# A decoder layer on one core: pre-formed weight sums paced by length, and one more pair split ahead of the last sums

## The chip, the cores and the metric

The kernel runs on one core of a Trainium2 chip. A core has TensorE (PE, the matrix unit; PEld is its weight load), VectorE (DVE), ScalarE (ACT), GpSimd (POOL) and SyncE (SP, which only issues transfers); 16 DMA engines move data between the device memory (HBM) and the on-chip memory. The metric is the device time of one execution in microseconds (us). Three executions of the kernel before took 1059.58, 1060.62 and 1060.71 us; the median is 1060.62.

## The reference

One layer on 256 tokens of 2048 numbers, all in float32:

```
h = rmsnorm(x, pre_mix_g);  proj = h @ w_in                        # 2048 x 4368
o_a = sliding-window attention (16 heads), o_b = forgetting attention (16 heads)
mix = [rmsnorm(o_a), rmsnorm(o_b)] @ w_out                          # 2048 x 2048
x = x + rmsnorm(mix, post_mix_g)
h = rmsnorm(x, pre_ffn_g)
gate, val = split(causal_dwconv(h @ w_up, conv_w, conv_b))          # 2048 x 11264
y = (gelu(gate) * val) @ w_down                                     # 5632 x 2048
out = x + rmsnorm(y, post_ffn_g)
```

## The kernel before, in words

**Weights.** They stream from HBM once, in raw tiles of 128 x 1024 float32 (512 KB, five buffers). TensorE multiplies in a reduced float32 format, so each raw tile is split in two: ACT casts it to a high half (`whi`), DVE subtracts that from the raw tile and writes the low half (`wlo`). This is a *split*; a product of two split numbers takes three matrix products (high x high, high x low, low x high) or, where both halves of the activations lie side by side, two. `w_load` issues the load of a raw tile on SP (L90) and counts it in `loads`.

**Stages.** (1) The input projection and both attentions, to about 290 us. (2) The output projection and the mixing norm: for each half of the tokens (t = 0, 1) DVE adds the two groups' products (L767), ACT squares and sums the result (L768), POOL multiplies it by the norm's gain (L769), POOL computes `rmix` = 1/rms with a power (L214), DVE adds the scaled mix to x (L787) and TensorE transposes the new x for the next projection (L794). (3) The up projection of the first 22 of 44 blocks of the feed-forward width, with convolution and gelu, then the down projection of these blocks in two passes over the output columns; then the same for the second 22 blocks. The end is the last norm.

**Weight sums.** In the down projection, six of eleven pairs of 128-row blocks per half (`FAST`) are multiplied with seven block products in place of eight (a Strassen scheme, `seven`). It needs sums of blocks of `w_down`. These sums are made in HBM in the background: `make_sums` gives, for each half and pair, eight steps. Four are plain copies (`put`, issued on SP, L80) and four are transfers that add into their destination (`add`, issued on POOL, L83). In the first half, the last four steps cover half as many columns. `w_load` issues these 96 steps in a fixed order: before, after the twelfth load, at five of every thirteen loads one step is taken off the list, whatever its length. During the passes no step is issued (`paused`).

**Order.** TensorE's order is written by hand. In stage (2) around the mixing norm, and in the passes, ACT and DVE (and POOL at the norm) also run in the order of the code; elsewhere a scheduler sets it. Instructions on one engine start in order, and a transfer issued on POOL waits in POOL's queue for what it reads.

**The last pass** (second half, columns 1024 to 2047) handles the pairs in the order 0, 2, 4, 1, 5, 6, 7, 3, 8, 9, 10. The last three (8, 9, 10: `HOLD`) are *held*: their products are done at the very end, output block by output block, so that each block's norm work can start early. After the last fast pair (7), `ahead` splits the next pairs, `add_early` adds the four early products on DVE (L1162 to L1169, the *early sums*), and then the remaining held pairs are split. POOL's gain multiplications (L1253) and DVE's last sums (L1240, L1229) follow.

Of the kernel before, what the change touches and what calls it, by code (L numbers as in the profile page):

```python
# [12 lines left out]
ALU = mybir.AluOpType  # L13
# [11 lines left out]
NEG = -1e30  # L25
FHALF = 22
HOLD = 3
SKIP = 12
FAST = (0, 2, 4, 5, 6, 7)


# [1 line left out]
def hybrid_layer(ctx: ExitStack, tc: tile.TileContext, x, pre_mix_g, w_in, b_forget, sinks,  # L33
# [3 lines left out]
    pe, act, dve, pool, sp = nc.tensor, nc.scalar, nc.vector, nc.gpsimd, nc.sync  # L37
# [12 lines left out]
    def bank(tag="acc"):  # L50
        return ps.tile([P, 512], F32, tag=tag, bufs=4, name="bank_" + tag)
# [13 lines left out]
    UNIT = 1024  # L65
    WB = 5

    pair_sums, sum_steps, loads, paused = {}, [], [0], [False]

    def make_sums(half, u):  # L70
        k = half * FHALF + 2 * u
        chunks = slice(0, 2) if half else slice(0, 1)
        t13, t24 = (tc.dram_tile([P, D], F32, name=n) for n in ("t13", "t24"))
        pair_sums[half, u] = t13, t24
        (t1, t3), (t2, t4), (b11, b12), (b21, b22) = (
            [w.rearrange("p (s x c) -> p s x c", s=2, x=2)[:, :, x, :] for x in range(2)]
            for w in (t13, t24, *(w_down[(k + a) * P:(k + a + 1) * P, :] for a in range(2))))

        def put(to, src, ch=slice(0, 2)):
            return lambda: sp.dma_start(to[:, ch, :], src[:, ch, :])  # L80

        def add(to, src, ch=slice(0, 2)):
            return lambda: pool.dma_start(to[:, ch, :], src[:, ch, :], accum_op=ALU.add)  # L83

        return [put(t1, b11), put(t3, b22), add(t1, b12), add(t3, b12), put(t2, b22, chunks),
                put(t4, b21, chunks), add(t2, t1, chunks), add(t4, t2, chunks)]

    def w_load(src, a, c, pin=False):
        raw = wp.tile([P, UNIT], F32, tag="raw", bufs=5, name="raw")
        i = sp.dma_start(raw[:, :a * c].rearrange("p (a c) -> p a c", a=a), src)  # L90
        if pin:
            tc.keep_in_program_order(i)
        loads[0] += 1
        if loads[0] > SKIP and loads[0] * 5 % 13 < 5 and sum_steps and not paused[0]:
            tc.keep_in_program_order(sum_steps.pop(0)())
        return raw, a, c

    last = []
# [55 lines left out]
    def w_rows(w, k0, a, c0, c):  # L154
        return w[k0 * P:(k0 + a) * P, c0:c0 + c].rearrange("(a p) c -> p a c", p=P)
# [190 lines left out]
    with tc.tile_pool(name="mixp", bufs=1) as mp:  # L346
# [407 lines left out]
        hold = tc.tile_pool(name="hold", bufs=1)  # L754
# [61 lines left out]
        def out_cols(n, t, cs):  # L816
            b = bank()
            for k, hi, lo in kept[n]:
# [7 lines left out]
        order = tc.manual_schedule(engines={mybir.EngineType.Activation, mybir.EngineType.DVE,  # L826
                                            mybir.EngineType.Pool})
# [50 lines left out]
    with tc.tile_pool(name="ffn", bufs=1) as fp:  # L878
# [132 lines left out]
        def product(b, lh, ll, rhs, cols, first, last, to=None):  # L1011
            hi, lo = rhs
            for i, (a, r) in enumerate(((lh, hi), (lh, lo), (ll, hi))):
                pe.matmul(b[:, to] if to else b, a, r[:, cols], start=(first and i == 0),  # L1014
                          stop=(last and i == 2))

        def column_pass(G, sums, weights, some, order, k00, c0, load, parts, hold=1):

            left, right = slice(0, 512), slice(512, UNIT)
            ready_sums = k00 or c0 == 0  # L1020
            fast = [u for u in order if u in some]
            plain = [u for u in order[:-hold] if u not in some]
            ready, started, held, banks = {}, set(), [], []

            def of(k, t):
                return G[k][:, t * P:(t + 1) * P], G[k][:, 256 + t * P:256 + (t + 1) * P]

            def first(bk):
                new = id(bk) not in started
                started.add(id(bk))  # L1030
                return new

            def prepare(u):
                k = k00 + 2 * u
                if u not in some:
                    return [parts(load(w_rows(w_down, k + a, 1, c0, UNIT)), UNIT)
                            for a in range(2)]
                b11 = parts(load(w_rows(w_down, k, 1, c0, 512)), 512)
                w13, w24 = (w[:, c0:c0 + UNIT].rearrange("p (a c) -> p a c", a=1)
                            for w in weights[u])  # L1040
                r13 = load(w13)
                r2 = load(w_rows(w_down, k + 1, 1, c0, UNIT))
                f13 = parts(r13, UNIT)
                if ready_sums:
                    r24 = load(w24)
                else:
                    r24 = r13
                    dve.tensor_tensor(r24[:, left], r2[:, right], r13[:, left], op=ALU.add)
                    dve.tensor_tensor(r24[:, right], r2[:, left], r24[:, left], op=ALU.add)
                b2 = parts(r2, UNIT)  # L1050
                return b11, f13, b2, parts(r24, UNIT)

            def ahead(*us):
                for u in us:
                    ready[u] = prepare(u)

            def seven(u, forms, m1, m5, m7, m6, p2, p3, p4):
                k, end = 2 * u, u == fast[-1]
                b11, f13, b2, f24 = forms

                def s_of(j):
                    return of(k, 1) if j == 3 else [sums[u][:, i * 384 + j * P:i * 384 + (j + 1) * P]
                                                    for i in range(2)]

                steps = [(m1, of(k, 0), b11, left), (m5, s_of(3), f13, left),
                         (m7, s_of(0), f13, right), (p2, of(k + 1, 0), b2, left),
                         (p3, s_of(2), b2, right), (m6, s_of(1), f24, left),
                         (p4, of(k + 1, 1), f24, right)]
                if u == fast[0]:
                    steps = steps[0:3] + steps[5:] + steps[3:5]  # L1070
                for bk, a, b, cols in steps:
                    product(bk, *a, b, cols, first(bk), end and bk in (m1, m5, m7, m6))

            def run(add_early):
                early, late = ([bank(tag) for _ in range(4)] for tag in ("acc", "att"))
                banks.extend(zip(late, (0, 0, 1, 1), (left, right, left, right)))
                for i, u in enumerate(order):
                    forms = ready.pop(u) if u in ready else prepare(u)
                    if u in some:
                        seven(u, forms, *early, *late[:3])  # L1080
                        if u == fast[-1]:
                            ahead(*order[i + 1:i + 3])
                            add_early(*early)
                    elif i >= len(order) - hold:
                        held.extend((2 * u + a, forms[a]) for a in range(2))
                    else:
                        for a in range(2):
                            for bk, t, cols in banks:
                                product(bk, *of(2 * u + a, t), forms[a], cols, first(bk),
                                        hold > 1 and bk is late[3] and a == 1 and  # L1090
                                        u == plain[-1])
                return late

            def block(i, bk=None, cols=None):
                b, t, c = banks[i]
                for n, (k, w) in enumerate(held):
                    product(bk or b, *of(k, t), w, cols or c, bk is not None and n == 0,
                            n == len(held) - 1, cols and slice(cols.start - 512, cols.stop - 512))

            return ahead, run, block  # L1100

        raw_turns, split_turns, cycles = [], [], [None, None]

        def load(src):
            if not raw_turns:
                raw_turns.extend(cycles[0])
            raw, c = raw_turns.pop(0), src.shape[-1]
            if raw is None:
                return w_load(src, 1, c)[0]
            sp.dma_start(raw[:, :c].rearrange("p (a c) -> p a c", a=1), src)  # L1110
            return raw

        def parts(src, n):
            if not split_turns:
                split_turns.extend(cycles[1])
            to = split_turns.pop(0)
            hi, lo = w_parts(n) if to is None else [x[:, :n] for x in to]
            split(hi, lo, src[:, :n])
            return hi, lo
# [53 lines left out]
        for half in range(2):  # L1173
# [5 lines left out]
            for g in range(FHALF // 2):  # L1179
# [36 lines left out]
                if g in FAST:  # L1216
                    i = FAST.index(g)
# [88 lines left out]
        for h in range(2):  # L1306
            if h:
                v = before_last(1, 4)
            b = bank()
# [38 lines left out]
```

## Time and profile before

| | |
|---|---|
| median of three executions | 1060.62 us |
| the profiled execution | 1059.58 us, of it 1057.9 us span from first to last instruction |
| granted TensorE clock, mean | 0.997 |
| busy: PE, DVE, ACT, POOL | 1043.1, 836.6, 651.9, 265.7 us |
| moved by DMA | 266.87 MB, mean 252 GB/s |
| background steps | 48 puts on SP, 48 adds on POOL |

In a time line or a chain, a row begins with the start and the duration in us; "x6" means that six like instructions are merged; the bracket at the end is the engine's idle time before it and what ended it. In a list of waits, a row says who waited for whom, for how long in total, how often, and the longest. A row of windows gives, after the stretch and its length, the busy time of PE, PEld, DVE, ACT and POOL (with counts), the granted clock, the DMA share and GB/s. Releasers are inferred.

### The profile page before, as it was taken

The numbers are of one execution on the slowest core, as the hardware profiler recorded it, in microseconds if no ns is written. First come the engines' busy times: TensorE is split into PE (matmuls) and PEld (weight loads), VectorE is DVE, ScalarE is ACT, GpSimd is POOL, SyncE is SP. The second block draws the span as 40 slices with busy tenths as digits, with TensorE's granted clock in tenths as the row PEclk, the third lists the DMA queues.
The fourth block names the chain that finished last, engine by engine and source line by source line (L and its number), as shares of the span: only waits on it lengthen the run. The fifth ranks groups of instructions, "written<-read, shape, count | busy, mean of one in ns | idle before, by whom it ended". The sixth has DMA issues, their size and how long they took to land.

```text
span 1057.9 us, 16559 instructions
## 1 busy us (share of the span) xinstructions
PE 1043.1 (99%) x5866; PEld 907.9 (86%) x5866; DVE 836.6 (79%) x1353; ACT 651.9 (62%) x1116; POOL 265.7 (25%) x304
## 2 busy tenths in 40 slices
PE   9999999999999999999999999999999999999995
PEld 7899988888888988888888888888888888888884
DVE  5989887887377797788796799857878788779885
ACT  6767667676466665665565666546555565558661
POOL 3254435442114132232231000013232231210005
PEclk9999999999999999999999999999999999999998
DMA  8768987977887999898989786879899897669792
GB/s 289 249 161 238 232 251 216 228 223 202 272 288 178 300 246 291 237 291 231 263 262 275 274 344 228 269 223 261 264 252 299 240 250 214 198 203 409 253 399 87
DMA packets 183806, 266.87 MB, mean 252 GB/s; under 512 B 9100, under 2 KB 133292, under 8 KB 182828
## 3 DMA queue, kind: packets, MB, share of 16 engines
q1 hardware_dynamic: 171200, 241.12, 69.0%
q0 software_dynamic: 11520, 22.02, 13.3%
q10 hardware_dynamic: 1004, 2.68, 0.7%
q8 instruction: 46, 0.75, 0.3%
q14 instruction: 36, 0.29, 0.1%
HBM read 261.45 MB, written 48.25 MB: 293 GB/s over the span
## 4 chain that ended last, share of the span: by engine, by line
PE 84%; DMA 5%; DVE 5%; issue 2%; ACT 2%; POOL 1%; SPq 0%; DVEq 0%; POOLq 0%; ACTq 0%
PE bank_acc L315 16%; PE bank_att L315 14%; PE bank_att L1014 11%; PE bank_acc L321 8%; PE bank_att L321 7%; PE bank_acc L284 7%; PE bank_acc L340 7%; PE bank_acc L1014 5%; PE bank_acc L289 4%; DMA raw<-in_w_out_dram 3%; PE bank_att L506 1%; DVE wlo L146 1%; PE bank_att L541 1%; DMA raw<-t 1%; PE bank_acc L977 1%
## 5 line engine op out<-in xcount | busy, mean ns | idle before, releaser
L146 DVE TENSOR_TENSOR wlo<-raw,whi 128x1024 fp32r<-128x1024 f32 (+3 forms) x271 | 336.6, 1254 | 109.0 <-ACT whi L143 101.1
L143 ACT CAST whi<-raw 128x1024 fp32r<-128x1024 f32 (+3 forms) x270 | 273.7, 1029 | 122.0 <-issue 42.7
L938 POOL TENSOR_TENSOR room<-room,rowf 128x256 f32<-128x256 f32 x88 | 96.5, 1116 | 357.6 <-DVE room L937 356.2
L315 PE MATMUL bank_acc<-hT,whi 128*128 128x512 f32 x736 | 173.3, 390 | 0.0
L315 PEld LDWEIGHTS bank_acc<-hT,whi 128*128 128x128 f32 x736 | 136.4, 188 | 27.4
L315 PE MATMUL bank_att<-hT,whi 128*128 128x512 f32 x640 | 150.6, 390 | 0.0
L315 PEld LDWEIGHTS bank_att<-hT,whi 128*128 128x128 f32 x640 | 118.7, 188 | 23.9
L1014 PE MATMUL bank_att<-whi,G 128*128 128x512 f32 x298 | 98.1, 389 | 0.0
L942 ACT ACTIVATE room<-room,cw 128x256 f32<-128x256 f32 x88 | 52.6, 601 | 67.5 <-POOL room L938 67.4
L321 PEld LDWEIGHTS bank_acc<-hT,wlo 128*128 128x128 f32 x736 | 89.3, 188 | 2.0
L321 PE MATMUL bank_acc<-hT,wlo 128*128 128x256 f32 x736 | 89.9, 279 | 0.0
L284 PE MATMUL bank_acc<-hT,whi 128*128 128x512 f32 x352 | 88.0, 395 | 0.0
L340 PE MATMUL bank_acc<-whi,oT 128*128 128x512 f32 (+1 forms) x272 | 81.8, 379 | 0.0
L321 PEld LDWEIGHTS bank_att<-hT,wlo 128*128 128x128 f32 x640 | 77.6, 188 | 1.7
L321 PE MATMUL bank_att<-hT,wlo 128*128 128x256 f32 x640 | 77.9, 279 | 0.0
L948 DVE SCALAR_TENSOR_TENSOR room<-room,cw 128x256 f32<-128x256 f32 x88 | 60.2, 687 | 18.3 <-ACT room L942 18.3
L344 DVE TENSOR_TENSOR wlo<-raw,whi 128x1024 fp32r<-128x1024 f32 (+1 forms) x61 | 66.7, 1117 | 8.8 <-ACT whi L343 7.8
L284 PEld LDWEIGHTS bank_acc<-hT,whi 128*128 128x128 f32 x352 | 63.3, 188 | 11.5
L343 ACT CAST whi<-raw 128x1024 fp32r<-128x1024 f32 (+1 forms) x61 | 57.5, 966 | 19.0 <-DMA raw<-in_w_down_dram 7.0
L1014 PEld LDWEIGHTS bank_att<-whi,G 128*128 128x128 f32 x298 | 55.9, 188 | 11.6
L340 PEld LDWEIGHTS bank_acc<-whi,oT 128*128 128x128 f32 x272 | 50.2, 188 | 9.4
L1014 PE MATMUL bank_att<-wlo,G 128*128 128x512 f32 x149 | 58.0, 389 | 0.0
(269 smaller groups left out, 1722.6 us busy)
## 6 DMA issues: line engine op xcount, KB each, us to landing
raw<-in_w_up_dram SPq DMA_DIRECT2D x176, 512.0 KB, 5.3
raw<-in_w_in_dram SPq DMA_DIRECT2D x51, 512.0 KB, 5.5
raw<-in_w_down_dram SPq DMA_DIRECT2D x49, 512.0 KB, 6.3
t<-in_w_down_dram SPq DMA_DIRECT2D x36, 512.0 KB, 6.9
raw<-in_w_out_dram SPq DMA_DIRECT2D x32, 512.0 KB, 6.9
t<-in_w_down_dram POOLq DMA_DIRECT2D x24, 512.0 KB, 10.8
raw<-t SPq DMA_DIRECT2D x18, 512.0 KB, 4.7
spare<-t SPq DMA_DIRECT2D x13, 512.0 KB
```

What stands on the lines that cost most here:

```text
L143: i1 = act.copy(hi[:, cs], raw[:, cs])
L146: i2 = dve.tensor_tensor(lo[:, cs], raw[:, cs], hi[:, cs].bitcast(F32), op=ALU.subtract)
L284: pe.matmul(b, parts[u][0][:, a, m * P:(m + 1) * P], hT[:, kt, :], start=(kt == 0), stop=(kt == KT - 1))
L315: pe.matmul(b, parts[u][0][:, a, m * P:(m + 1) * P], hT[:, kt, :], start=(kt == 0), stop=(kt == KT - 1))
L321: pe.matmul(b[:, 256:512], parts[u][1][:, a, m * P:(m + 1) * P], hT[:, kt, 0:256], start=False, stop=False)
L340: pe.matmul(b, a, r[:, cols], start=(first and i == 0), stop=(last and i == 2))
L343: act.copy(hi, src)
L344: dve.tensor_tensor(lo, src, hi.bitcast(F32), op=ALU.subtract)
L938: pool.tensor_tensor(u[:, 2:258], u[:, 2:258], rowf, op=ALU.mult)
L942: act.activation(y, u[:, 2:258], AF.Identity, bias=cw[:, 3, ch:ch + 1], scale=cw[:, 2, ch:ch + 1])
L948: dve.scalar_tensor_tensor(y, u[:, 1:257], cw[:, 1, ch:ch + 1], y, op0=ALU.mult, op1=ALU.add)
L1014: pe.matmul(b[:, to] if to else b, a, r[:, cols], start=(first and i == 0), stop=(last and i == 2))
```

## The change

Three things change.

1. Each step now has a size: a put the number of its 256 KB column chunks (2, or 1 for the short ones), an add twice that. Each load adds 9/8 to a credit, and steps are issued while the credit covers the next one's size.
2. No credit is given for loads 1 to 12 (as before) and 91 to 112. The latter are the second half of the output projection, the first tiles of the up projection and the mixing norm.
3. In the last pass `ahead` splits three pairs (3, 8, 9) before the early sums, where it split two (3, 8). The other passes keep two.

```diff
-SKIP = 12
+QUIET = ((0, 12), (90, 112))
+PACE = 9 / 16
...
         def put(to, src, ch=slice(0, 2)):
-            return lambda: sp.dma_start(to[:, ch, :], src[:, ch, :])
+            return ch.stop, lambda: sp.dma_start(to[:, ch, :], src[:, ch, :])

         def add(to, src, ch=slice(0, 2)):
-            return lambda: pool.dma_start(to[:, ch, :], src[:, ch, :], accum_op=ALU.add)
+            return 2 * ch.stop, lambda: pool.dma_start(to[:, ch, :], src[:, ch, :],
+                                                       accum_op=ALU.add)
...
         loads[0] += 1
-        if loads[0] > SKIP and loads[0] * 5 % 13 < 5 and sum_steps and not paused[0]:
-            tc.keep_in_program_order(sum_steps.pop(0)())
+        if not paused[0] and not any(a < loads[0] <= b for a, b in QUIET):
+            owed[0] += 2 * PACE
+            while sum_steps and owed[0] >= sum_steps[0][0]:
+                size, step = sum_steps.pop(0)
+                owed[0] -= size
+                tc.keep_in_program_order(step())
...
                         if u == fast[-1]:
-                            ahead(*order[i + 1:i + 3])
+                            ahead(*order[i + 1:i + (4 if hold > 1 else 3)])
                             add_early(*early)
```

Six lines are added above most of the code, so a line of the kernel before has a number lower by up to six than the same line after.

TensorE's order is the same in both kernels. POOL's order at the mixing norm, before (`t_80` to `t_82` are the sums in HBM; `rg` the 1/rms of an attention group):

```order
L83 DMA t_80<-in_w_down_dram 256x512
L214 TENSOR_TENSOR rg_3429<-rv,mhalf 128x1
L214 TENSOR_TENSOR rg_3433<-rv,mhalf 128x1
L83 DMA t_81<-t_80 128x512
L769 TENSOR_TENSOR mix_sb<-mix_sb,gbc_mix 128x512 x4
L83 DMA t_81<-t_81 128x512
L83 DMA t_82<-in_w_down_dram 256x512 x2
L769 TENSOR_TENSOR mix_sb<-mix_sb,gbc_mix 128x512 x2
L214 TENSOR_TENSOR rmix_3818<-rv,mhalf 128x1
```

and after:

```order
L84 DMA t_81<-t_80 128x512
L84 DMA t_81<-t_81 128x512
L590 TENSOR_TENSOR sqs<-sqs,sqo 128x256 x3
L84 DMA t_82<-in_w_down_dram 256x512
L220 TENSOR_TENSOR rg_3436<-rv,mhalf 128x1
L220 TENSOR_TENSOR rg_3440<-rv,mhalf 128x1
L84 DMA t_82<-in_w_down_dram 256x512
L775 TENSOR_TENSOR mix_sb<-mix_sb,gbc_mix 128x512 x6
L220 TENSOR_TENSOR rmix_3820<-rv,mhalf 128x1
```

The three adds that stood between the fourth and the fifth gain multiplication now stand ahead of the first.

POOL's order in the attention stage, from the last tables of the sliding-window heads on, before:

```order
L83 DMA t_76<-in_w_down_dram 256x512 x2
L584 TENSOR_TENSOR sqs<-sqs,sqo 128x256
L83 DMA t_75<-t_75 128x512
L584 TENSOR_TENSOR sqs<-sqs,sqo 128x256 x2
L473 TENSOR_TENSOR scr<-scr 128x256 x2
```

and after:

```order
L84 DMA t_76<-in_w_down_dram 256x512
L590 TENSOR_TENSOR sqs<-sqs,sqo 128x256
L84 DMA t_76<-in_w_down_dram 256x512
L84 DMA t_77<-t_76 128x512
L590 TENSOR_TENSOR sqs<-sqs,sqo 128x256 x2
L479 TENSOR_TENSOR scr<-scr 128x256 x2
L84 DMA t_77<-t_77 128x512
```

An add that reads what the add right ahead of it writes (`t_77<-t_76`) now stands behind it in the queue.

DVE's order near the end of the last pass, before (`slots`, `more` and `wlo` are places for low halves):

```order
L344 TENSOR_TENSOR wlo<-raw,whi 128x1024 x2
L1162 TENSOR_TENSOR y_sb<-s,y_sb 128x512
L1163 TENSOR_TENSOR s<-bank_acc,s 128x512
...
L1169 TENSOR_TENSOR y_sb<-s,y_sb 128x512
L344 TENSOR_TENSOR wlo<-raw,whi 128x1024
L344 TENSOR_TENSOR slots<-raw,slots 128x1024
L344 TENSOR_TENSOR more<-raw,more 128x1024
L344 TENSOR_TENSOR more<-spare,more 128x1024
```

and after:

```order
L350 TENSOR_TENSOR wlo<-raw,whi 128x1024 x3
L350 TENSOR_TENSOR slots<-raw,slots 128x1024
L1168 TENSOR_TENSOR y_sb<-s,y_sb 128x512
L1169 TENSOR_TENSOR s<-bank_acc,s 128x512
...
L1175 TENSOR_TENSOR y_sb<-s,y_sb 128x512
L350 TENSOR_TENSOR more<-raw,more 128x1024
L350 TENSOR_TENSOR more<-spare,more 128x1024
```

Pair 9's two splits (`wlo`, `slots`) moved from behind the eight early sums to ahead of them; ACT's two casts for them moved ahead of its copy for the first sum.

More of the change, by code (lines that the diff above doesn't have):

```diff
@@ L66, in hybrid_layer @@
     WB = 5
-    pair_sums, sum_steps, loads, paused = {}, [], [0], [False]
+    pair_sums, sum_steps, loads, owed, paused = {}, [], [0], [0.0], [False]
     def make_sums(half, u):
```

## The prediction

> **What bounds the kernel now.** I read the page first (busy shares), then the waits of TensorE, then the time line around each of those waits, and the DMA rows last.
>
> ```profile
> PE 1043.1 (99%) x5866; PEld 907.9 (86%) x5866; DVE 836.6 (79%) x1353; ACT 651.9 (62%) x1116; POOL 265.7 (25%) x304
> ...
> PE bank_acc L200 <- DVE junk L195: 1.3, 1, 1.3
> PE bank_att L1014 <- DVE more L344: 1.2, 1, 1.2
> PE bank_acc L365 <- DMA x_in<-in_x_dram: 0.9, 1, 0.9
> PE bank_att L794 <- DVE x_sb L787: 0.6, 1, 0.6
> PE bank_att L553 <- DVE pl L344: 0.5, 1, 0.5
> PE bank_att L365 <- DMA x_in<-in_x_dram: 0.4, 1, 0.4
> ```
>
> TensorE works for 1043.1 of 1057.9 us. Its waits add up to 4.9 us, and none in the middle is for a weight load: only the two on `x_in`, 1.3 us at the start, wait for a DMA. So no copy or accumulation for the weight sums holds TensorE directly; it can do so only through VectorE (DVE) or GpSimd (POOL). Two waits lie at places the change touches: 0.6 us at L794 (mixing norm) and 1.2 us at L1014 (last pass). With 0.5 us at L553 they are all that a new order of steps could give back, 2.3 us and a little for restarting: the gain is bounded near 0.25%.
>
> **The mixing norm.** The time line of PE, DVE, ACT and POOL there:
>
> ```profile
> 324.56 0.39 PE L340 MATMUL bank_acc<-whi,oT 128*128 128x512 f32 x1
> 325.58 1.32 PE L794 MATMUL bank_att<-ident,x_sb 128*128 128x128 f32 x8 [0.63 <-DVE x_sb L787]
> ...
> 329.61 1.04 PE L794 MATMUL bank_att<-ident,x_sb 128*128 128x128 f32 x8
> ...
> 321.89 0.16 DVE L212 TENSOR_SCALAR rv<-st_m 128x1 f32<-128x1 f32 x1
> ...
> 324.77 2.74 DVE L787 SCALAR_TENSOR_TENSOR x_sb<-mix_sb,rmix,x_sb 128x512 f32<-128x512 f32 x4 [2.72 <-POOL rmix L214]
> ...
> 320.94 0.63 ACT L768 ACTIVATE junk<-mix_sb 128x512 bf16<-128x512 f32 x1 [2.02 <-DVE mix_sb L767]
> ...
> 316.54 2.55 POOL L769 TENSOR_TENSOR mix_sb<-mix_sb,gbc_mix 128x512 f32<-128x512 f32 x2 [7.52 <-ACT junk L768]
> 319.04 0.80 POOL L83 DMA_DIRECT2D t<-t  x1
> 319.59 2.06 POOL L83 DMA_DIRECT2D t<-in_w_down_dram  x2
> 320.72 3.50 POOL L769 TENSOR_TENSOR mix_sb<-mix_sb,gbc_mix 128x512 f32<-128x512 f32 x2
> 323.23 1.51 POOL L214 TENSOR_TENSOR rmix<-rv,mhalf 128x1 f32<-128x1 f32 x1
> ...
> 336.32 0.55 POOL L214 TENSOR_TENSOR rmix<-rv,mhalf 128x1 f32<-128x1 f32 x1
> ```
>
> The input of `rmix` is ready at 321.89 + 0.16 = 322.05, but POOL ends it at 324.74, because three accumulations (L83) stand ahead of two gain multiplications, which then run up to 323.2 or later. DVE waits 2.72 us, and TensorE 0.63 us behind it.
>
> The change puts no step there: the three accumulations leave this place (the puts of these loads too). The third multiplication can then start at 316.54 + 2.55 = 319.09 and takes 1.27 (2.55 / 2), to 320.4. The fourth must let ACT read the same columns first (320.94 + 0.63 = 321.57), so it ends near 322.85; `rmix` at its undisturbed 0.55 ends at 323.4, where it was 324.74. So L787 starts 1.3 us earlier, at 323.45, and its first quarter (2.74 / 4 = 0.7) is done at 324.15. TensorE asks for it at 324.56 + 0.22 = 324.8 (0.22 us is its pace for 512 columns, below). The 0.63 us go, and the 1.32 us of eight transposes become the 1.04 us of the next eight: **0.9 us** in all. What is late next is the second half of the rows, one `rmix` later; its DVE work follows L787 and moves forward by the same 1.3 us, more than TensorE does, so no new wait opens. Bounds: 0, if another input of L787 is late, and 0.9, since TensorE loses no more here; I take 0.9, all of it, because POOL's part is so plainly the last.
>
> Elsewhere in this stage one weight split moves ahead of the evacuations at L767. It delays a bank by 1.2 us (the split's duration below), and TensorE has 48 other products (10 us) before it wants the bank: nothing.
>
> **The last pass.** The rows of its end, PE, DVE, ACT and POOL, and a piece of the chain:
>
> ```profile
> 1032.70 1.09 PE L1014 MATMUL bank_att<-more,G 128*128 128x512 f32 x4
> ...
> 1034.95 0.74 PE L1014 MATMUL bank_att<-more,G 128*128 128x512 f32 x2 [1.15 <-DVE more L344]
> ...
> 1021.15 2.48 DVE L344 TENSOR_TENSOR wlo<-raw,whi 128x1024 fp32r<-128x1024 f32 x2
> ...
> 1023.54 0.69 DVE L1162 TENSOR_TENSOR y_sb<-s,y_sb 128x512 f32<-128x512 f32 x1
> ...
> 1029.17 1.22 DVE L344 TENSOR_TENSOR wlo<-raw,whi 128x1024 fp32r<-128x1024 f32 x1
> ...
> 1031.44 1.22 DVE L344 TENSOR_TENSOR more<-raw,more 128x1024 fp32r<-128x1024 f32 x1
> 1032.58 2.31 DVE L344 TENSOR_TENSOR more<-spare,more 128x1024 fp32r<-128x1024 f32 x1
> ...
> 1031.89 4.15 POOL L1253 TENSOR_TENSOR y_sb<-y_sb,gbc_ffn 128x512 f32<-128x512 f32 x2 [94.61 <-DMA gbc_ffn<-in_post_ffn_g_dram]
> ...
> 1021.31 1.05 ACT L343 CAST whi<-raw 128x1024 fp32r<-128x1024 f32 x1 [0.20 <-DMA raw<-in_w_down_dram]
> ...
> 1026.30 1.05 ACT L343 CAST more<-spare 128x1024 fp32r<-128x1024 f32 x1 [0.20 <-DMA spare<-in_w_down_dram]
> ...
> 1014.27 6.94 DMA raw<-in_w_down_dram
> ```
>
> TensorE waits for the low half of the very last tile, pair 10's second (`more<-spare`, ends 1034.89). Between 1021.15 and then DVE is never idle: pair 8's splits, eight sums (1023.54 to 1029.17, 5.63 us), pair 9's two splits, pair 10's two. The change moves pair 9's splits in front of the sums. It takes no work off DVE ahead of pair 10, so the tile that TensorE waits for comes no earlier: **gain 0**. Pair 9 itself was not waited for.
>
> There is a small loss. Pair 8's last tile lands at 1014.27 + 6.94 = 1021.21 and pair 10's last near 1026.3, four tiles later, so tiles land 1.27 us apart: pair 9's at about 1022.5 and 1023.75. Ahead of the sums, DVE would split them as they come: ACT's cast of the second ends near 1024.85 (1.05), and its split starts then, where back to back it would start at 1023.54 + 1.14 = 1024.7 (two splits take 1031.44 - 1029.17 = 2.27 us). The sums and pair 10 slip by **0.2 us**; bounds 0 (casts hidden) and 0.5 (both tiles late by a quarter).
>
> Why does the last split take 2.31 us, when the one before takes 1.22? POOL's first gain multiplication became ready at 1031.89 inside the earlier split, and ran between the two: 1.09 us, nearly all of the 1.15 us wait. By the Trainium skill, GPSIMD Engine Reference, section "8. Key points", POOL shares its SBUF interfaces with VectorE and contends with instructions that have two SBUF inputs; the trace agrees (2.31 against 1.22 us; both splits read two SBUF tiles). By that rule the wait depends on which split POOL catches, which is a rival below.
>
> **The new pace of the steps.** From the rule in the code, in units of a 256 KB put (an accumulation counts double): loads 13 to 90 carried 68 units and now 86; loads 91 to 112 20 and now 0; the rest of the first half 84 and now 92; the second half 80 and now 74. All 252 are still issued before a pass needs them.
>
> ```profile
> q1 hardware_dynamic: 171200, 241.12, 69.0%
> q0 software_dynamic: 11520, 22.02, 13.3%
> ...
> 40.00:290.00 250.00, 249.46 (x1550) 221.42 (x1550) 196.54 (x441) 166.94 (x368) 97.59 (x121) 1.00 0.81 226
> ...
> 346.00:580.00 234.00, 234.00 (x1373) 207.28 (x1372) 186.40 (x291) 141.74 (x230) 60.58 (x60) 1.00 0.93 269
> ...
> 280.00:300.00 20.00, 20.00 (x90) 16.57 (x89) 7.23 (x6) 6.57 (x8) 0.00 (x0) 1.00 1.01 329
> ...
> L80 SPq DMA_DIRECT2D t<-in_w_down_dram x48: 496/507/2131, 32.1 to 837.6; - x48
> ```
>
> Accumulations (q0) took 0.133 x 1057.9 = 141 us for 168 units, 0.84 us each; plain transfers 730 us for 241 MB, 0.79 us per unit. So 18 more units before load 90 raise the DMA share of 40 to 290 from 0.81 to 0.87, and 8 more that of 346 to 580 from 0.93 to 0.96. The window at 1.01 passed without a wait of TensorE: 90 products in 20 us, 0.22 us each, is its pace. Five raw tiles, each worth 12 products of 512 columns (2.7 us), lie between a load and its use. On SyncE's queue a put takes 0.5 us to issue, against those 2.7 us per load, so no load behind it is late; puts move by a few loads and none is added. I cost the new pace at **0**; if that cover were gone, the 8 units are 6.5 us.
>
> On POOL's queue some accumulations now follow directly the one they read: the second must wait for a landing.
>
> ```profile
> 107.95 0.85 POOL L597 TENSOR_SCALAR p<-scr 128x256 f32<-128x256 f32 x1 [10.27 <-DVE wlo L146]
> ...
> DMA to landing us min/median/max: 4.6/8.7/15.2
> ...
> 118.91 1.45 POOL L83 DMA_DIRECT2D t<-t  x1
> ...
> 140.15 0.74 POOL L584 TENSOR_TENSOR sqs<-sqs,sqo 128x256 f32<-128x256 f32 x1 [16.34 <-ACT sqo L577]
> ```
>
> At the place of 118.91 the accumulation would hold POOL for a landing (8.7, at most 15.2 us), to some 128 or 134. Behind it stand one sum of squares (L584), which nothing needs before the next one, and the work of 140.15 on, ahead of which POOL idles 16.34 us. The other such place is near 92; what is queued behind it starts at 107.95, after 10.27 us of idling. Cost 0, with at least 6 us to spare.
>
> **Sum.** 1059.58 us is the profiled execution (span 1057.9 and 1.7 around it): -0.9 + 0.2 + 0 = 1058.9. The median shown, 1060.62, lies 1.04 above that execution, so I predict **1059.9**.
>
> **The rivals.**
> 1. Both waits go. If the gain rows land later relative to DVE, POOL starts after the last split began (past 1032.6), and that split takes 1.22 us. For it: the wait is made of POOL's 1.09 us. Against: the loads ahead of those rows keep their order. -0.9 - 1.15 - 0.1 gives 1058.4.
> 2. Slower: POOL catches pair 10's first split as well. It does if that split starts after 1031.89; it starts at 1031.44 now and 1031.65 by my sum, so 0.25 us decide. POOL's first multiplication then runs ahead of it and the second ahead of the last split, one more 1.1 us beside the slip of 0.2 to 0.9: +2.0 at the last pass and -0.9 at the norm, 1061.7.
> 3. A held POOL queue or fuller DMA starves VectorE in the attention stage. For it: the new adjacent accumulations; against: the idle times above. 3 to 6.5 us: 1064.
> 4. The norm's wait stays (another input of L787 is last): 1060.62 + 0.2 = 1060.8.
>
> **Chances.** Forecast 0.52, rivals 0.16, 0.17, 0.08, 0.07. A difference of 0.2% (2.1 us) is about what a measurement can tell from none. Faster by more: rival 1, and 0.04 of the forecast, as runs of one kernel differ by 1.1 us: 0.20. Slower by more: rival 3 and 0.03 of rival 2: 0.11. Within: 0.69. The forecast's own range is 1059.2 to 1060.5; with rivals 1, 2 and 4 it is 1058.2 to 1061.8.
>
> **What would show it.** Right: no wait of TensorE at the transposes near 325, `rmix` right behind the fourth multiplication, and the last pass still with about 1.2 to 1.5 us of wait for `more<-spare`, that split still over 2 us. Wrong: that wait gone (rival 1) or near 3 us with pair 10's first split over 2 us (rival 2); a new wait between 40 and 300 for `ql`, `keys` or `pl`, or for `wlo` anywhere (rival 3).

## The result and the profile after

The changed kernel is slower by about a quarter of a per cent, a small step but clear of the noise: 1062.14 us median (1059.85 to 1067.1, 22 runs) against 1059.92 us (1058.51 to 1061.79, 22 runs) for the kernel before, ratio 1.0024, 95% interval 1.0014 to 1.0034. Its runs also spread twice as far. The profiled execution is one of the long ones, 1066.02 us with a span of 1064.3, 6.4 us over the 1057.9 of before; the sum of its waits need not be the typical one.

The busy row of the page and TensorE's waits, after:

```profile
PE 1046.6 (98%) x5866; PEld 911.5 (86%) x5866; DVE 837.3 (79%) x1353; ACT 651.0 (61%) x1116; POOL 266.8 (25%) x304
...
PE bank_att L512 <- DVE scr L567: 1.6, 1, 1.6
PE bank_att L327 <- DVE wlo L152: 1.4, 1, 1.4
PE bank_acc L206 <- DVE junk L201: 1.3, 1, 1.3
PE bank_att L559 <- DVE pl L350: 1.3, 1, 1.3
PE bank_att L1020 <- DVE more L350: 1.2, 1, 1.2
PE bank_att L571 <- DVE pl L350: 0.8, 1, 0.8
PE bank_acc L371 <- DMA x_in<-in_x_dram: 0.4, 1, 0.4
```

The waits add up to 8.0 us where they were 4.9. The one at the mixing norm (0.6) is gone and the one of the last pass (1.2) has stayed. New are 1.6 us for `scr` (L567) and 1.4 us for `wlo` (L152); that for `pl` (L559) has grown from 0.5 to 1.3, and a second of 0.8 has joined it (L571). Those for `x_in` at the start are 0.9 us shorter. The other 3.5 us are in the busy row: the same 5866 products took 1046.6 us instead of 1043.1.

**The mixing norm**, time line of POOL, DVE and PE, after:

```profile
327.40 1.29 POOL L775 TENSOR_TENSOR mix_sb<-mix_sb,gbc_mix 128x512 f32<-128x512 f32 x1 [3.33 <-ACT junk L774]
328.65 0.56 POOL L220 TENSOR_TENSOR rmix<-rv,mhalf 128x1 f32<-128x1 f32 x1
...
329.24 2.74 DVE L793 SCALAR_TENSOR_TENSOR x_sb<-mix_sb,rmix,x_sb 128x512 f32<-128x512 f32 x4 [1.54 <-POOL rmix L220]
...
331.00 1.03 PE L800 MATMUL bank_att<-ident,x_sb 128*128 128x128 f32 x8
```

`rmix` stands right behind the last gain multiplication, DVE waits 1.54 instead of 2.72 us for it, and TensorE's transposes start without a wait and take 1.03 us.

**The last pass**, DVE, POOL and PE, after:

```profile
1037.85 1.22 DVE L350 TENSOR_TENSOR more<-raw,more 128x1024 fp32r<-128x1024 f32 x1
1038.99 2.32 DVE L350 TENSOR_TENSOR more<-spare,more 128x1024 fp32r<-128x1024 f32 x1
...
1038.02 4.43 POOL L1259 TENSOR_TENSOR y_sb<-y_sb,gbc_ffn 128x512 f32<-128x512 f32 x2 [94.36 <-DMA gbc_ffn<-in_post_ffn_g_dram]
...
1041.36 0.72 PE L1020 MATMUL bank_att<-more,G 128*128 128x512 f32 x2 [1.18 <-DVE more L350]
```

POOL's multiplication begins inside the same split as before, pair 10's first (1.22 us), and lengthens the last (2.32). The wait is 1.18 us against 1.15.

**The attention stage, first place.** POOL, ACT, DVE and PE, after:

```profile
77.26 2.15 POOL L479 TENSOR_TENSOR scr<-scr 128x256 f32<-128x256 f32 x2 [6.08 <-DVE es L526]
79.35 2.04 POOL L84 DMA_DIRECT2D t<-in_w_down_dram  x2
...
92.71 0.84 ACT L149 CAST whi<-raw 128x768 fp32r<-128x768 f32 x1 [3.34 <-DMA raw<-in_w_in_dram]
...
93.58 0.96 DVE L152 TENSOR_TENSOR wlo<-raw,whi 128x768 fp32r<-128x768 f32 x1 [3.60 <-ACT whi L149]
...
97.50 1.14 DVE L686 SCALAR_TENSOR_TENSOR vpb<-bank_acc,rpre,vpb 128x384 fp32r<-128x384 f32 x2
98.56 0.95 DVE L152 TENSOR_TENSOR wlo<-raw,whi 128x768 fp32r<-128x768 f32 x1
99.42 0.84 DVE L567 TENSOR_TENSOR scr<-bank_att,olow 64x256 f32<-64x256 f32 x2
...
100.41 0.35 PE L512 MATMUL bank_att<-keys,qh 64*128 64x256 f32 x1 [1.59 <-DVE scr L567]
```

Two accumulations of 512 KB are issued as a pair at 79.35. ACT then waits 3.34 us for a weight tile, DVE 3.60 us for the cast. When the tiles come, DVE has splits and two evacuations of `vpb` to do at once, and the evacuation that TensorE needs (L567) stands behind them. In the kernel before these two accumulations are issued 12.6 us apart, on either side of POOL's wait for `es`:

```profile
66.04 1.12 POOL L83 DMA_DIRECT2D t<-in_w_down_dram  x1
...
78.64 0.90 POOL L83 DMA_DIRECT2D t<-in_w_down_dram  x1
```

The windows of 4 us (busy us of PE, PEld, DVE, ACT and POOL, then granted clock, DMA share and GB/s), first before:

```profile
76.00:80.00 4.00, 4.00 (x25) 4.00 (x24) 3.79 (x12) 3.07 (x10) 3.00 (x3) 1.00 0.30 72
84.00:88.00 4.00, 4.00 (x27) 3.91 (x26) 2.97 (x6) 2.42 (x5) 3.67 (x4) 1.00 1.00 307
92.00:96.00 4.00, 4.00 (x25) 3.91 (x24) 3.99 (x6) 2.98 (x5) 0.51 (x1) 1.00 1.07 248
```

and after:

```profile
76.00:80.00 4.00, 4.00 (x25) 4.00 (x24) 3.79 (x13) 3.05 (x11) 2.74 (x3) 1.00 0.06 17
84.00:88.00 4.00, 4.00 (x27) 3.91 (x26) 3.09 (x5) 1.86 (x4) 3.70 (x5) 1.00 0.98 146
92.00:96.00 4.00, 4.00 (x25) 3.91 (x24) 0.96 (x1) 1.07 (x2) 0.38 (x1) 1.00 1.08 347
```

The DMA engines are idle at 76 to 80 (share 0.06) and full from 84 on in both. But after, the full engines move 146 GB/s at 84 to 88 where they moved 307, with both accumulations of the pair in flight. A single accumulation brings such a window too (before, 80 to 84: share 0.87, 165 GB/s); the pair makes two of them in a row (after, 80 to 84: 0.89, 167). DVE is left with 0.96 us of work out of 4 at 92 to 96, where it had 3.99. TensorE is still busy there; it pays three microseconds later.

**The clock behind that wait**, windows of the kernel after (granted clock third from the right):

```profile
98.00:100.40 2.40, 0.81 (x13) 0.64 (x12) 2.35 (x6) 1.79 (x4) 0.81 (x1) 1.00 0.84 254
...
102.00:105.50 3.50, 3.50 (x14) 3.50 (x13) 3.04 (x13) 1.98 (x10) 0.00 (x0) 0.52 0.96 241
```

From 102.0 to 105.5 TensorE ran at 0.52 of its clock: 3.5 x 0.48 = 1.7 us lost behind a wait of 1.6, and counted as busy. This is half of what the busy row has grown by. The other half is at the very start, ahead of any step, and no work of the change: up to 17.38 us TensorE was busy for 15.74 us, and in the profile before it did the same products by 16.67 us in 14.08. With the shorter waits for `x_in` 0.7 of the 6.4 us are lost there.

**Second place.** POOL, DVE and PE near 134, after:

```profile
122.53 1.21 POOL L84 DMA_DIRECT2D t<-in_w_down_dram  x1
134.20 0.81 POOL L84 DMA_DIRECT2D t<-t  x1 [10.46 <-DMA t<-in_w_down_dram]
134.75 1.02 POOL L590 TENSOR_TENSOR sqs<-sqs,sqo 128x256 f32<-128x256 f32 x1
...
134.39 2.19 DVE L537 TENSOR_SCALAR p<-p,rs 128x256 f32<-128x256 f32 x4
...
139.77 0.50 PE L559 MATMUL bank_att<-pl,vpa 128*128 128x512 f32 x1 [1.26 <-DVE pl L350]
```

An accumulation that reads the one ahead of it holds POOL for 10.46 us, until 134.20. Then it and the sum of squares behind it run together with L537, whose four pieces take 2.19 us. These pieces lie on the way to `pl`, which TensorE awaits. In the kernel before POOL idles beside them:

```profile
130.68 1.01 DVE L531 TENSOR_SCALAR p<-p,rs 128x256 f32<-128x256 f32 x4
```

**Third place.** ACT's queue, POOL, ACT and PE near 357, after:

```profile
356.81 0.53 ACTq L997 DMA_DIRECT2D x_dram<-x_sb  x1
...
358.41 0.86 POOL L84 DMA_DIRECT2D t<-t  x1
...
370.77 1.05 ACT L149 CAST whi<-raw 128x1024 fp32r<-128x1024 f32 x1 [2.38 <-DMA raw<-in_w_up_dram]
...
373.13 1.08 PE L327 MATMUL bank_att<-hT,wlo 128*128 128x256 f32 x7 [1.43 <-DVE wlo L152]
```

The first accumulation behind the norm is issued 1.6 us after the second of two writes of `x` (1 MB each), and a weight tile comes late 12 us on.

### The profile page after: what moved, and what is told of

The parts are those of the page before. It is cut to its first block, busy times and chain, and to the rows that moved or that the text cites. A ratio compares the mean times of both kernels' runs of the same rounds, so it can differ in the third digit from the quotient of the medians.

```text
span 1064.3 us, 16565 instructions
## 1 busy us (share of the span) xinstructions
PE 1046.6 (98%) x5866; PEld 911.5 (86%) x5866; DVE 837.3 (79%) x1353; ACT 651.0 (61%) x1116; POOL 266.8 (25%) x304
## 4 chain that ended last, share of the span: by engine, by line
PE 81%; DVE 7%; DMA 6%; ACT 2%; issue 2%; POOL 1%; DVEq 0%; SPq 0%; POOLq 0%; ACTq 0%
PE bank_acc L321 15%; PE bank_att L321 13%; PE bank_acc L346 12%; PE bank_acc L327 8%; PE bank_att L1020 7%; PE bank_acc L290 7%; PE bank_att L327 7%; PE bank_acc L295 4%; PE bank_acc L1020 3%; DMA raw<-in_w_down_dram 2%; DMA raw<-in_w_up_dram 2%; DMA raw<-t 1%; DVE wlo L152 1%; DVE more L350 1%; PE bank_att L512 1%
## 5 line engine op out<-in xcount | busy, mean ns | idle before, releaser
L152 DVE TENSOR_TENSOR wlo<-raw,whi 128x1024 fp32r<-128x1024 f32 (+3 forms) x271 | 333.7, 1243 | 114.5 <-ACT whi L149 108.7
```

What stands on the lines that cost most here:

```text
L152: i2 = dve.tensor_tensor(lo[:, cs], raw[:, cs], hi[:, cs].bitcast(F32), op=ALU.subtract)
```

## The experiments

Each ratio is to runs of the kernel before on the same chip.

### One part at a time

The three parts of the change alone, and the two without the pace. Edits against the kernel before:

```diff
 norm_quiet, quiet_ahead
-        if loads[0] > SKIP and loads[0] * 5 % 13 < 5 and sum_steps and not paused[0]:
+        if (loads[0] > SKIP and not 90 < loads[0] <= 112 and loads[0] * 5 % 13 < 5
+                and sum_steps and not paused[0]):
 three_ahead, quiet_ahead
-                            ahead(*order[i + 1:i + 3])
+                            ahead(*order[i + 1:i + (4 if hold > 1 else 3)])
 pace_only: the kernel after with
-QUIET = ((0, 12), (90, 112))
+QUIET = ((0, 12),)
-                            ahead(*order[i + 1:i + (4 if hold > 1 else 3)])
+                            ahead(*order[i + 1:i + 3])
```

Under the old rule the free window pushes one of the 96 steps, the last accumulation, past the last load, so `norm_quiet` and `quiet_ahead` leave it out.

> The kernel before, with its old rule of steps (5 of 13 loads); only loads 91 to 112 issue no step. Theory A (the new pace is what costs; the mixing norm gains as predicted): TensorE's wait of 0.6 us at the norm's transposes is gone and the median falls by 0.5 to 1.0 us, to about 1059.2. Theory B (keeping the norm's window free costs, because its steps crowd the places behind it): the median rises by 1 us or more. Theory C (the last pass costs): as A.

> The kernel before, with three pairs instead of two split ahead of the early sums in the last pass, and nothing else. Theory A: within 0.3 us of the kernel before; the wait for the last tile of the last pass stays at 1.1 to 1.5 us. Theory C (the third pair costs: GpSimd's first gain multiplication catches another split in some executions): the median rises by 1 to 2 us, and the wait there is near 3 us.

> The kernel before with both other parts of the change (no step at loads 91 to 112, three pairs ahead) but the old rule of 5 loads in 13. Theory A: 0.5 to 1.0 us under the kernel before, about 1059.2, and about 3 us under the changed kernel. Theories B and C: 1 to 2 us above the kernel before.

> The changed kernel with its new pace alone: steps also at loads 91 to 112, two pairs ahead as before. Theory A (the new pace puts more and other accumulations into the attention stage; their late landings and GpSimd work that runs beside VectorE hold TensorE): slower than the kernel before by 2 to 4 us, 1062 to 1064, with new waits of about 1 us each between 90 and 300 us. Theories B and C: within 1 us of the kernel before.

| run | median us | ratio | 95% interval |
|---|---|---|---|
| norm_quiet | 1058.36 | 0.9992 | 0.9982 to 1.0001 |
| three_ahead | 1061.24 | 1.0008 | 0.9995 to 1.0020 |
| quiet_ahead | 1058.45 | 0.9987 | 0.9976 to 0.9997 |
| pace_only | 1067.58 | 1.0071 | 1.0058 to 1.0084 |

The loss is the pace's; the other two parts together gain. `pace_only` is far slower than any theory said, because the new pace puts two accumulations among the norm's gain multiplications. POOL and PE there, in `pace_only`:

```profile
326.73 1.78 POOL L84 DMA_DIRECT2D t<-in_w_down_dram  x2
327.88 3.16 POOL L775 TENSOR_TENSOR mix_sb<-mix_sb,gbc_mix 128x512 f32<-128x512 f32 x2
330.73 0.83 POOL L220 TENSOR_TENSOR rmix<-rv,mhalf 128x1 f32<-128x1 f32 x1
...
PE bank_att L800 <- DVE x_sb L793: 3.0, 2, 2.8
```

That is the mechanism of the norm again, 2.8 us instead of 0.6. So the free window is worth more under the new pace than under the old.

### Without the missing step

`quiet_done` and `quiet_done_ahead` are the first and third kernel above with all 96 steps: the old rule is 5 loads of 12 behind load 200.

```diff
-                and loads[0] * 5 % 13 < 5
+                and loads[0] * 5 % (13 if loads[0] <= 200 else 12) < 5
```

> The kernel before with the norm's window free; the old rule, but 5 loads in 12 behind load 200, so that all 96 steps are issued. Theory A: 0.5 to 1.2 us under the kernel before, ratio 0.999, the norm's wait gone.

> The same with three pairs ahead. If the third pair costs nothing: as the kernel with two pairs, within 0.4 us. If it costs (ratio 1.0008 alone): 0.5 to 1 us above it, with another wait of 0.3 us for a tile of pair 10 in the last pass.

0.9987 (0.9978 to 0.9996) with two pairs, 1058.89 us, and 0.9985 (0.9975 to 0.9994) with three, 1058.45 us. The third pair costs nothing measurable (three_ahead's 1.0008 had 1.000 in its interval). `quiet_done_ahead` beats both kernels: it is the change without the new pace.

### Where the pace costs

```diff
 pace_quiet: the kernel after with
-                            ahead(*order[i + 1:i + (4 if hold > 1 else 3)])
+                            ahead(*order[i + 1:i + 3])
 old_early: up to load 90; old_late: behind load 112; more_old: up to load 90, with 6 instead of 5
+            if loads[0] <= 90:
+                if loads[0] * 5 % 13 < 5 and sum_steps:
+                    tc.keep_in_program_order(sum_steps.pop(0)[1]())
+            else:
                 owed[0] += 2 * PACE
 phase
-owed, paused = {}, [], [0], [0.0], [False]
+owed, paused = {}, [], [0], [-3.0], [False]
 low_early, and mid_early with 1 / 2
-            owed[0] += 2 * PACE
+            owed[0] += 2 * (PACE if loads[0] > 112 else 7 / 16)
```

> The changed kernel with two pairs ahead again: the new pace and the free norm alone. Theory A (the pace costs, the third pair nothing): as the changed kernel, 1062 to 1063, 2 to 3 us above the kernel before. Theory C (the third pair costs near 1 us, since alone it stood at a ratio of 1.0008): about 1061, 1 us under the changed kernel.

> The changed kernel with the old rule (5 loads in 13) up to load 90 and the new pace behind load 112. Theory D (the steps of the first 90 loads cost: more of them beside the first attention blocks, with the waits of 1.6, 1.3 and 0.8 us at 99, 137 and 238 us and the slower clock behind the first): these waits go and the time is within 0.5 us of the kernel before with the norm's window free, 1058.5 to 1059.5. Theory E (the pace behind the norm costs, by the wait of 1.4 us for `wlo` at 370 us and others like it): still 1061 to 1063.

> The changed kernel with the new pace up to load 90 and the old rule behind load 112. Theory D: as the changed kernel, 1061 to 1063. Theory E: 1058.5 to 1059.5, as the kernel before with the norm's window free.

> The changed kernel, its pace unchanged, but every step two to three loads later (the account starts at -3 units). Theory F (the amount of traffic costs: 86 units instead of 68 by load 90): as the changed kernel, within 0.7 us of it. Theory G (single places cost: an accumulation that meets a landing or VectorE work at a bad moment): the waits stand at other places and add up to another sum, so the median moves by 1 us or more in either direction.

> The changed kernel with 7/16 instead of 9/16 up to load 90: spread by length, but only the 68 units there that the kernel before has. Theory F (the amount before load 90 costs): as the changed kernel with the old rule up to load 90, 1058.9, within 0.7 us. Theory G (the places cost): other places than either, so 1060 to 1063, with a wait over 1 us somewhere between 90 and 300 us.

> The changed kernel with 8/16 up to load 90: 78 units there, between the 68 of 7/16 (ratio 0.9993) and the 86 to 88 of 9/16 (1.0024). Theory F (amount): between them, ratio 1.000 to 1.0015. Theory G (places): anything from 0.999 to 1.004, with a wait over 1 us at a place that neither of the two has.

> The changed kernel with the old way of placing steps up to load 90, one step at a load whatever its size, but at 6 loads of 13 instead of 5 (some 82 units instead of 68). Theory F: ratio 1.001 to 1.003, so near the changed kernel, though the spacing is the old one. Theory G (the new places cost): as with 5 of 13, 0.9985 to 1.0000.

| run | rule up to load 90 | units there | median us | ratio | 95% interval |
|---|---|---|---|---|---|
| pace_quiet | 9/16 | 86 | 1063.86 | 1.0030 | 1.0016 to 1.0043 |
| phase | 9/16, later | 84 | 1062.25 | 1.0024 | 1.0014 to 1.0034 |
| old_late | 9/16 (old behind 112) | 86 | 1061.34 | 1.0008 | 0.9999 to 1.0017 |
| mid_early | 8/16 | 76 | 1064.25 | 1.0044 | 1.0032 to 1.0057 |
| low_early | 7/16 | 68 | 1060.29 | 0.9993 | 0.9979 to 1.0007 |
| old_early | 5 of 13 | 68 | 1058.89 | 0.9994 | 0.9983 to 1.0004 |
| more_old | 6 of 13 | 84 | 1058.65 | 0.9988 | 0.9979 to 0.9996 |

(Units are counted from the rule.) `pace_quiet`, `phase`, `old_early` and `low_early` spoke for the amount (theory F): what has 84 to 86 units is slow, what has 68 is not; `old_late`, with 86, lies between. `mid_early` and `more_old` end that. 84 units placed by the old rule cost nothing, and 76 placed by the new rule cost most. Nor is it the new rule behind load 112 as such: `more_old` and `old_early` use it. It is where single steps fall (theory G). TensorE's waits of `more_old` behind the start, no more than these two:

```profile
PE bank_att L1024 <- DVE more L354: 0.8, 1, 0.8
...
PE bank_att L563 <- DVE pl L354: 0.6, 1, 0.6
```

### Through what a step acts

```diff
 no_hold: the kernel after with
-                put(t4, b21, chunks), add(t2, t1, chunks), add(t4, t2, chunks)]
+                put(t4, b21, chunks), add(t2, b12, chunks), add(t4, b21, chunks)]
 tiny
+                c = slice(0, 64 if loads[0] <= 90 else 512)
+                return pool.dma_start(to[:, ch, c], src[:, ch, c], accum_op=ALU.add)
 aside
+            aside = tc.dram_tile([P, 2, 512], F32, name="aside")
...
+                if loads[0] <= 90:
+                    return sp.dma_start(aside[:, ch, :], b12[:, ch, :])
```

> The changed kernel, but the two later accumulations of each pair of sums add a piece of `w_down` instead of the sum accumulated just before (so two of the four sums of a pair are others than the reference's); bytes and places in the rule of loads stay, but GpSimd no longer waits for one accumulation's landing before it issues the next. Theory H (the held GpSimd queue costs: released late, the accumulation and the sum of squares behind it run beside VectorE's work on the path near 134 us): the wait at 137 us falls from 1.3 to about 0.5 us and the median by 0.7 to 1.5 us, to about 1061; the wait at 98 us stays. Theory I (only the crowd of transfers costs): within 0.5 us of the changed kernel, the wait at 137 us stays.

> The changed kernel, but the accumulations issued up to load 90 move 64 of 512 columns (their sums stay incomplete): GpSimd issues as many as before at the same places, the DMA engines move an eighth of their bytes. Theory K (bytes: the weight tiles land late because the DMA engines are full there): the waits at 98, 137 and 238 us shrink below 0.6 us each and the time falls by 2 to 3.5 us against the changed kernel, ratio to the kernel before 0.998 to 0.9995. Theory L (GpSimd's side: the issue and what stands behind it collide with VectorE): as the changed kernel, ratio 1.002 to 1.003.

> The changed kernel, but each accumulation issued up to load 90 is a plain copy of the same size, from `w_down` to a place that nothing reads, issued by SyncE (those sums stay incomplete). The bytes written stay, GpSimd issues nothing there. Theory K: still slower than the kernel before, ratio 1.001 or more, with waits behind late weight tiles. Theory L: ratio 0.998 to 0.9995.

`no_hold`: 1.0036 (1.0020 to 1.0053), no faster. POOL's 10.46 us are gone and with them the second place: its wait for `pl` at L559 is back at 0.5. But the accumulations that were held are issued earlier, at 120 and 122 us, and the steps behind them meet other work: a wait of 1.2 us at L571 has come, near 182. Its waits:

```profile
PE bank_att L571 <- DVE pl L350: 1.2, 1, 1.2
...
PE bank_att L559 <- DVE pl L350: 0.8, 2, 0.5
```

`tiny`: 0.9997 (0.9987 to 1.0008), 0.0027 or 2.9 us under the kernel after, with no new wait over 0.3 us left: GpSimd's issues at the same places do no harm without their bytes. (With the bytes the holds of POOL's queue shrink too, near 97 from 6.55 to 2.40 us.) `aside`: 1.0004 (0.9995 to 1.0012), so below the 1.001 that theory K wanted. The same amount as plain copies brings no new wait in the attention stage; what is left is 1.8 us for `wlo` at 366, the third place. So it takes accumulations of the full size. Whether their kind matters, or only the moment at which POOL lets them go, `aside` does not separate: SP issues its copies where the rule puts them, the first two of 512 KB at 47 and 59 us, while POOL issued the accumulations at 79 and 80. The windows speak for the kind, without proving it: at 84 to 88 the full engines moved 298 GB/s in `aside`, with plain copies in flight, and 146 in the kernel after.

### One accumulation moved by one load

Every kernel with the wait for `scr` at 98 has the pair at 79 and 80 us (six of them), and of the others so far only `tiny` has it. One step decides it, the first accumulation: at load 19 POOL issues it ahead of its wait for `es`, at load 20 behind it. `one_early` takes it out of the pair in the kernel after; `one_late` puts it into the pair in the kernel before. POOL's order differs by this one row, and the orders of the other four engines are the same as in the kernel each is made from.

```diff
 one_early: the kernel after with
-            while sum_steps and owed[0] >= sum_steps[0][0]:
+            while sum_steps and owed[0] + (loads[0] == 19) / 8 >= sum_steps[0][0]:
 one_late: the kernel before with
-        if loads[0] > SKIP and loads[0] * 5 % 13 < 5 and sum_steps and not paused[0]:
+        if (loads[0] > SKIP and (loads[0] * 5 % 13 < 5) != (loads[0] in (19, 20))
+                and sum_steps and not paused[0]):
```

> The changed kernel with one step, the first accumulation, at load 19 instead of 20. This lets GpSimd issue it ahead of a group of its own work, near 66 us, instead of directly ahead of the second at 79 and 80 us; nothing else moves on any engine. Theory M (this pair is what costs: it crowds out the weight tiles of 84 to 100 us): the wait at 98 us falls below 0.5 us, no slow clock behind it, and the time falls by 1 to 2.5 us against the changed kernel: ratio to the kernel before 0.9995 to 1.0012. Theory N (it is one bad place among many): as the changed kernel within 0.6 us.

> The kernel before with its first accumulation at load 20 instead of 19, which makes the same pair at 79 and 80 us; nothing else moves on any engine. Theory M: slower by 0.7 to 2 us, with a wait for `scr` near 98 us that the kernel before doesn't have. Theory N: within 0.5 us, no such wait.

`one_early`: 1060.33 us, 1.0009 (0.9998 to 1.0021), where the kernel after stood at 1.0024. `one_late`: 1061.48 us, 1.0013 (1.0001 to 1.0026). Their waits, `one_early`:

```profile
PE bank_att L1020 <- DVE more L350: 2.4, 2, 1.3
PE bank_att L327 <- DVE wlo L152: 1.6, 1, 1.6
...
PE bank_att L559 <- DVE pl L350: 1.1, 1, 1.1
PE bank_att L571 <- DVE pl L350: 1.0, 1, 1.0
```

and `one_late`:

```profile
PE bank_att L553 <- DVE pl L344: 1.7, 2, 1.1
...
PE bank_att L321 <- DVE wlo L146: 0.5, 1, 0.5
```

In `one_early` the wait for `scr` is gone. In `one_late` there is a new one of 1.1 us; it stands at 112 and for `pl`, not at 98 for `scr` as theory M had said. The starved windows are the same: 189 GB/s at 84 to 88 and 1.08 us of DVE work out of 4 at 88 to 92. But `phase`, with one accumulation at 80 us and no pair, waits 1.1 us at the same place, so the pair is not the only way to this wait. One accumulation, one load earlier or later, is worth 1.4 to 1.6 us either way (0.0013 and 0.0015 of 1060, uncertain by 1.3 and 1.6). Theory M holds for about two fifths of what the pace costs; the rest is put down to the second and third places below. The profiled execution of `one_early`, 1064.85 us, has something else besides: in the last pass TensorE waits for both tiles of pair 10, 1.18 and 1.25 us.

**The sum.** `quiet_done_ahead` (0.9985) and the kernel after (1.0024) differ in the rule of steps alone: 0.0039, or 4.1 us. The pair is 1.6 us by `one_early`. `old_late` lies 0.0016, 1.7 us, under the kernel after; its first accumulation behind the norm comes 12.5 us after the writes of `x`, not 1.6, and its profile has no wait for `wlo`. The held accumulation is 0.7 us by its wait (1.26 to 0.55 in `no_hold`). That makes 4.0. The close agreement is luck: the first two terms are differences of ratios and uncertain by about 1.5 us each, and the third is a wait, whose removal did not make `no_hold` faster. The third place was not tested alone. For it: of the ten profiles with an accumulation within 2 us behind these writes, six have the wait (0.5 to 1.8 us); of the ten with it over 10 us behind, none. Four of the first ten, the kernel before among them, do without, so what else has to come together there stays open.

## Why the prediction was wrong

- **Mixing norm, -0.9 us: right.** The wait is gone, `rmix` stands right behind the fourth multiplication, the transposes take 1.03 us. Without the pace the window gives 0.9987 (`quiet_done`), 1.4 us (0.4 to 2.3).
- **Last pass, gain 0, loss 0.2: right in the profile after.** The wait went from 1.15 to 1.18 us; two and three pairs ahead measure alike (0.9987 and 0.9985). Rival 1 (that wait goes) and rival 2 (POOL catches pair 10's first split) did not happen there. The part can cost more than its bound of 0.5 all the same: in `one_early` pair 9's tiles came late, pair 10's first split began at 1035.16 and TensorE waited 1.18 us for it too, without POOL lengthening it (1.22 us). Some second wait for pair 10 is in five of the twenty profiles, with two pairs ahead and with three.
- **New pace of the steps, 0: this step failed**, and with it the sign of the sum. The prediction raised the DMA share of 40 to 290 us from 0.81 to 0.87 and found room, with five raw tiles as cover and a full window (1.01) that had passed without a wait. But the average hides windows of 4 us: those shown above lie between 0.30 and 1.07 before and between 0.06 and 1.08 after. And the cover did not hold: ACT waited 3.34 us for a tile. It put this term at 0, and the rule of steps measured 4.1 us. The full window that it looked at lies in the output projection, where DVE has 7.23 us of work in 20; over 40 to 290 us it has 196.54 in 250. What an added step costs depends on the window that it falls in, and the accumulations do not fall where the rule of loads puts them but where POOL's queue lets them go: two that the rule spaces three loads apart came out 0.8 us apart. The amount, which the prediction costed (18 more units), was not the matter: 84 units by the old rule are free.
- **The adjacent accumulations on POOL, 0 with 6 us to spare: failed.** The hold was sized well (10.46 us, predicted 8.7 to 15.2) and nothing that waits for POOL was late. The cost is on DVE: what the hold releases runs beside the softmax scaling, 0.7 us of wait (the whole kernel was no faster without the hold). The prediction asked who waits behind the held instruction, not whom it meets when it is let go. The same page of the Trainium skill that it cited for the last pass (GPSIMD Engine Reference, "8. Key points") says that POOL shares its SBUF interfaces with VectorE, and limits the contention to certain VectorE instructions. The trace agrees that there is one (2.19 us beside POOL's work, 1.01 without); whether L537 is an instruction of the kind that the page means, no run here shows.
- **Rival 3**, a held POOL queue or fuller DMA that starves VectorE in attention, was the case, at the places named (`pl`, `wlo`) and one more (`scr`). Its chance was 0.08; its price, 3 to 6.5 us to a time of 1064, fits the long runs (1064 to 1067), while by the ratios the median lost 4.1 us to the pace and got 1.6 back from the rest.
- **The base.** The sum starts from the median of three executions, 1060.62; over 22 it is 1059.92. By its own terms the forecast would have been 1059.2, so the real miss is 2.9 us and not 2.2. (Rival 1's time is 1058.5 by its own terms, not 1058.4.)

## What to carry to other kernels

A share of DMA time over 250 us says nothing on one more transfer: look at windows of 4 us, and at what the transfer's issuing queue does just before, since an in-order queue turns steps that are spaced in the program into a bunch. Where an order is spread by a rule of counts, read the order that comes out on the issuing engine, and look for equal rows that stand together (`x2`). When a rule change costs time, first test whether amount or place is the cause: two settings of the new rule and a denser one of the old separated them here.

## What the runs showed of the hardware

- A wait of TensorE can cost twice. Behind 1.6 us at 99 us, among small products (0.81 us of work in 2.40), the granted clock fell to 0.50 for 3.41 us (1.7 us lost). Five of the twenty profiles have one such stretch ahead of the end, always of the same length and always 0.2 to 1.7 us behind a wait: of 1.6 us in the kernel after, 1.95 in `mid_early`, 2.81 in `pace_only`, 1.18 and 1.25 close together in `one_early`, 1.26 in `three_ahead`. In `mid_early` and in `one_early`:

```profile
115.68:119.09 3.41, 3.41 (x18) 3.41 (x17) 3.37 (x7) 1.77 (x4) 1.61 (x2) 0.50 0.89 296
...
1038.85:1042.26 3.41, 3.41 (x9) 2.63 (x9) 1.35 (x4) 0.72 (x2) 1.87 (x2) 0.50 0.02 5
```

  The length of the wait does not decide it: 1.83 us at 366 in `aside` and 1.65 at 367 in `one_early` had none behind them, nor had those of 1.2 to 1.4 us at 139, 372 and 1040 in the kernel after. So the loss of a wait is not proportional to it, which helps to spread the runs: of the changed kernel's 22 runs the six at a mean clock of 0.994 or 0.995 took 1062.87 to 1067.1 us, the eight at 0.997 took 1060.12 to 1063.16. It is not all of the spread, as two at 0.998 took 1064.3. One such stretch costs as much as the pair of accumulations, so a single execution cannot tell such changes apart. The Trainium skill, TensorE: Matmul & The Clock Gate, section "HAM oscillation — how this bites in real kernels", gives idle gaps over some 3.4 us as the limit; here waits of 1.2 to 2.8 us stood ahead of the slow stretches. By its section "What's actually happening" the window is free-running, which would make it a matter of luck; no run here tests that.
- An accumulation's issue followed at once by a small POOL addition stretched the DVE instruction that it met by 1.2 us (L537 near 134: 2.19 us for four pieces that take 1.01 in `no_hold` and before).
